# A fifth pair of high and low weight tiles, and a smaller scratch for GpSimd's DMA descriptors

## The chip, the cores and the metric

The kernel runs on one core of one Trainium2 chip. The metric is the time of one execution in microseconds (us) on the device. A core has five engines, each with an instruction stream of its own that it works through in the order written: TensorE (PE in the profile, with PEld for its loads of stationary weights), VectorE (DVE), ScalarE (ACT), GpSimd (POOL) and SyncE (SP), which here only issues DMAs. Engines wait for each other through semaphores. Matmul results go to PSUM; weights and activations lie in SBUF, on chip.

## The reference

Two layers of a decoder trunk on 256 tokens of width 1024, all in float32. Each layer normalizes x, projects it, runs four causal token mixers side by side (stick-breaking attention, RWKV-7, block attention with rotary embedding, HGRN2), gates their projected outputs and adds an output projection, then a SwiGLU feed-forward part:

```python
for layer in range(DEPTH):
    h = rms_norm(x, norm1_g[layer])
    y_sb, y_rwkv, y_moba, y_hgrn = four_mixers(h @ w_in[layer])   # each (256, 256)
    merged = None
    for n, y_n in enumerate((y_sb, y_rwkv, y_moba, y_hgrn)):
        gate = jax.nn.sigmoid(cols(GATE_OFF + n * D_MODEL, D_MODEL))
        term = gate * (y_n @ w_branch[layer, n])
        merged = term if merged is None else merged + term
    x = x + merged @ w_out[layer]
    h2 = rms_norm(x, norm2_g[layer])
    x = x + (jax.nn.silu(h2 @ w_ffn_gate[layer]) * (h2 @ w_ffn_up[layer])) @ w_ffn_down[layer]
return rms_norm(x, final_g)
```

The RWKV-7 recurrence is computed in two chunks of 128 steps per head. Each chunk needs the inverse of a unit triangular 128x128 matrix; the kernel builds it up from blocks of 16.

## The kernel before, in words

**Weights.** Every weight matrix is read once, in tiles of 128x1024 (512 KB). SyncE issues a load into one of four `raw` tiles (L133). A matmul on full float32 is replaced by three on a shorter format: ScalarE rounds the tile to a high part `hi` (L128), VectorE subtracts to get the low part `lo` (L129), and TensorE adds hi·h_hi, hi·h_lo and lo·h_hi (`mm3`, recorded under L80). One pair of hi and lo tiles therefore stands between the two splitting engines and TensorE; the pool has `spl` such pairs, four before. A pair is free again when TensorE's last matmul with that weight tile is done. Some weights are split ahead of their stage into tiles of other pools (`prefetch`, names c and y).

**Stages.** A layer runs through `phase` (projections, mixers, gates and branch projections), `merge` (the output projection) and `ffn`. In `phase` the work comes as units (projections, gate and branch tiles, which keep TensorE busy) and streams (the mixers, whose short steps alternate between engines). `drive` interleaves them by a running estimate of TensorE's time; that estimate counts matmuls alone and does not read the pools' sizes. The order on each engine is then settled when the program is built: the framework places instructions engine by engine as buffers and inputs become available in its own plan, so the number of buffers can change the order on ScalarE, VectorE and SyncE. Once built, the order is fixed.

**PSUM.** Projections and gates accumulate into `pa`, of which there are three. Each is released by the engine that reads it last: for HGRN2's last projection (`use_n`) ScalarE copies one half (L810), takes the sigmoid of the other (L811), and VectorE multiplies (L812), which frees the buffer. A gate's `pa` is freed by ScalarE's sigmoid (L1011); a branch's `pa` by VectorE's multiplication with the gate (L1029, L1031).

**The inverse.** VectorE fills the triangular matrices LB by predicated copies (L542). GpSimd sends each chunk to DRAM (L548, tensor `flat`), ScalarE's queue fetches the diagonal blocks of 16 back with one matrix to a partition (L564), VectorE inverts them in three levels of multiplications and sums (L591, L594, tile `yb`), GpSimd sends the result to DRAM (L599, `tri`) and ScalarE's queue fetches it back (L602). L602 waits, in ScalarE's stream, for the landing of `tri`. GpSimd issues six DMAs in the whole program, four to `flat` and two to `tri`. For GpSimd's DMAs the descriptors are written by software into a scratch at the bottom of SBUF; its size per partition is an argument of the program's constructor and is 16384 bytes where none is given.

Of the kernel before, what the change touches and what calls it, by code (L numbers as in the profile page):

```python
# [39 lines left out]
SWAP = [*range(8, 16), *range(8), *range(16, 32)]  # L40
P_MU, P_W0, P_A0, P_KK, P_KA, P_RK, P_V0, P_LB, NPAR = 0, 8, 10, 12, 14, 16, 18, 20, 24

NB = dict(raw=4, spl=4, h4=2, p=11, y=8, c1=8, xy=4, b1=5, c2=4, b2=2, h1=4, h2=3, gt=4, pa=3, p1=2, p2=2, p3=1)


@with_exitstack
def trunk(ctx, tc, x, w_t, w_n, w_br, w_out, w_gu, w_dn, par, lora, rows, gains, consts, masks, out):
# [9 lines left out]
    def sb(tag, width, dt=F32):  # L57
        return mx.tile([128, width], dt, name=tag, tag=tag, bufs=NB[tag])

    def ps(tag):  # L60
        return psum.tile([128, 512], F32, name=tag, tag=tag, bufs=NB[tag])

# [68 lines left out]
    def load_raw(src):  # L131
        raw = sb("raw", 1024)
        nc.sync.dma_start(raw, src)  # L133
        return raw
# [3 lines left out]
    def weight(key):  # L138
        name, idx = key[0], key[1:]
        raw = early.pop(key, None)  # L140
        if raw is None:
            raw = load_raw(WSRC[name][idx])
        w = (mx.tile([128, 1024], F32R, name="hi", tag="hi", bufs=NB["spl"]),
             mx.tile([128, 1024], F32R, name="lo", tag="lo", bufs=NB["spl"]))
        if guard and guard[2]:
# [860 lines left out]
    def gate_unit(h, l, n, f, gt):  # L1006
        gt[n, f] = []

        def use(t, p):
            g = sb("gt", 512)  # L1010
            nc.scalar.activation(g, p, AF.Sigmoid)  # L1011
            gt[n, f].append(g)
        return proj_N(h, [("n", l, 2 + 2 * n + f, c) for c in range(4)], use)

    def branch_unit(l, n, f, cnt, yT, gt, mg, mT):
        i = cnt[f]
        cnt[f] += 1
        w = weight(("br", l, n, f))
        y = yT[n][0]
        gs = gt.pop((n, f))  # L1020
        for t in range(2):
            p = ps("pa")
            for hp in range(2):
                mm3(p, (y[0][:, hp, t * 128:(t + 1) * 128], y[1][:, hp, t * 128:(t + 1) * 128]),
                    cut(w, slice(hp * 512, (hp + 1) * 512)), hp == 0, hp == 1)
            g = gs[t]
            if i == 0:
                mg[f, t] = sb("p", 512)
                nc.vector.tensor_tensor(mg[f, t], g, p, op=OP.mult)  # L1029
            else:  # L1030
                nc.vector.tensor_tensor(g, g, p, op=OP.mult)  # L1031
                e = nc.vector if i == 3 else nc.gpsimd
                e.tensor_tensor(mg[f, t], mg[f, t], g, op=OP.add)  # L1033
            if t == 0 and f == 1 and i == 3:
                assert cnt[0] == 4
                yield from flip_unit(0, mg, mT)
            yield
# [13 lines left out]
    def phase(hr, g, l, ws):  # L1051
# [4 lines left out]
        def add(gen, ready=yes):  # L1056
            units.append((ready, gen))
# [39 lines left out]
        for n in (0, 2, 3, 1):  # L1097
            for f in range(2):
                add(lambda n=n, f=f: gate_unit(h, l, n, f, gt), lambda: len(gt) < NB["gt"] // 2)
                add(lambda n=n, f=f: branch_unit(l, n, f, cnt, yT, gt, mg, mT),  # L1100
# [195 lines left out]
```

## Time and profile before

| | |
|---|---|
| three runs | 924.91, 926.62, 926.95 us; median 926.62 |
| profiled execution | 924.23 us, of which 922.4 us from the first to the last instruction |
| TensorE busy | 905.6 us (98%), 5902 matmuls |
| VectorE busy | 650.8 us (71%) |
| ScalarE busy | 475.4 us (52%) |
| GpSimd busy | 88.2 us (10%) |
| DMA | 158.11 MB, mean 171 GB/s; mean granted TensorE clock 0.998 |

In the rows of a timeline the columns are: start in us from the span's start, length in us, engine and line, operation, tiles (written <- read), shape, and the number of merged instructions; in brackets the idle time of the engine before it and what ended that. An engine name with q is its sequencer, which issues a DMA and leaves the engine idle. A matmul's row says which tile is moving and which is stationary: `pa<-hi,h` moves a hi tile through stationary h. Matmuls overlap and their ends are modelled, so the distance of starts is the better measure there. In a table of waits the columns are who waited for whom, the sum in us, how often, and the longest.

### The profile page before, as it was taken

To read this page: it belongs to the slowest core of one execution; us is meant where nothing else is said; L and a number is where in the kernel's file an instruction comes from. 1 tells how busy PE (TensorE), PEld (TensorE's weight loads), DVE (VectorE), ACT (ScalarE), POOL (GpSimd) and SP (SyncE) were. 2 spreads that over 40 slices of the span, in tenths; PEclk is the share of its full clock that TensorE was granted. 3 is DMA by queue.
4 is the path that set the end of the run, shared out by engine and by line. 5 is a ranking of instruction groups with operands and counts; after the bars stand their busy time and mean duration, and the time that the engine had idled before them with its cause. 6 is when DMAs were issued, how large, how long until landed. Compare 5 with 4: busy or idle time off the path is not lost.

```text
span 922.4 us, 15005 instructions
## 1 busy us (share of the span) xinstructions
PE 905.6 (98%) x5902; PEld 758.9 (82%) x5902; DVE 650.8 (71%) x957; ACT 475.4 (52%) x726; POOL 88.2 (10%) x100
## 2 busy tenths in 40 slices
PE   8999999999999999999999999999999999999996
PEld 5999777778788888888889987777788888888885
DVE  6667877887766666668567778768778566666665
ACT  6564385345635445556355646644455445545453
POOL 3012100323000000000000211033130000000000
PEclk9999999999999999999999999999999999999999
DMA  8644453435754565567434544533377356556551
GB/s 311 221 149 152 121 174 126 135 131 184 257 199 140 181 198 189 183 208 268 141 116 160 163 138 152 174 104 117 116 218 256 106 188 207 191 182 192 183 183 46
DMA packets 48536, 158.11 MB, mean 171 GB/s; under 512 B 9393, under 2 KB 9777, under 8 KB 48466
## 3 DMA queue, kind: packets, MB, share of 16 engines
q1 hardware_dynamic: 43632, 155.19, 51.6%
q10 hardware_dynamic: 4450, 0.79, 0.5%
q0 software_dynamic: 384, 1.18, 0.4%
q8 instruction: 46, 0.75, 0.3%
q14 instruction: 24, 0.20, 0.1%
HBM read 154.91 MB, written 2.23 MB: 170 GB/s over the span
## 4 chain that ended last, share of the span: by engine, by line
PE 84%; DVE 9%; issue 2%; ACT 2%; DMA 1%; POOL 1%; ACTq 0%; POOLq 0%; DVEq 0%
PE pa L80 58%; PE p L80 23%; DVE lo L129 2%; PE pa L89 1%; PE p L89 1%; DVE b L542 1%; ACT hi L128 1%; DMA flat<-b 1%; DVE b L867 1%; DVE b L965 1%; DMA raw<-in_w_out_dram 1%; PE pa L196 0%; DVE xy L591 0%; DVE c L981 0%; DVE c L980 0%
## 5 line engine op out<-in xcount | busy, mean ns | idle before, releaser
L129 DVE TENSOR_TENSOR lo<-raw,hi 128x1024 fp32r<-128x1024 f32 x268 | 330.9, 1240 | 154.5 <-ACT hi L128 150.9
L128 ACT CAST hi<-raw 128x1024 fp32r<-128x1024 f32 x268 | 279.3, 1049 | 234.3 <-PE pa L80 109.3
L80 PE MATMUL pa<-h,hi 128*128 128x256 f32 (+1 forms) x1280 | 278.0, 339 | 0.0
L80 PEld LDWEIGHTS pa<-h,hi 128*128 128x128 f32 x1280 | 216.1, 190 | 24.5 <-issue 2.0
L80 PE MATMUL pa<-hi,h 128*128 128x512 f32 x576 | 193.2, 400 | 3.1 <-DVE p L812 3.1
L80 PE MATMUL pa<-h,lo 128*128 128x256 f32 x960 | 180.1, 283 | 0.0
L80 PEld LDWEIGHTS pa<-h,lo 128*128 128x128 f32 x960 | 148.8, 191 | 6.9 <-issue 0.7
L80 PEld LDWEIGHTS pa<-hi,h 128*128 128x128 f32 x576 | 108.2, 188 | 29.6 <-DVE p L812 4.0
L80 PE MATMUL p<-hi,c 128*128 128x512 f32 (+1 forms) x352 | 113.5, 394 | 0.0
L80 PE MATMUL pa<-lo,h 128*128 128x512 f32 x288 | 112.9, 392 | 0.0
L80 PEld LDWEIGHTS p<-hi,c 128*128 128x128 f32 x352 | 66.1, 189 | 15.1 <-DVE c L129 0.6
L80 PE MATMUL p<-lo,c 128*128 128x512 f32 (+1 forms) x176 | 69.3, 394 | 0.0
L80 PEld LDWEIGHTS pa<-lo,h 128*128 128x128 f32 x288 | 54.2, 188 | 9.6
L263 POOL TENSOR_TENSOR rs<-rs,half 128x1 f32<-128x1 f32 x10 | 5.9, 594 | 471.4 <-DVE rs L262 471.4
L80 PE MATMUL pa<-hi,y 128*128 128x512 f32 x128 | 44.0, 399 | 0.1
L80 PE MATMUL p<-hi,b 128*128 128x512 f32 x128 | 41.6, 396 | 0.3 <-DVE b L129 0.2
L80 PEld LDWEIGHTS p<-lo,c 128*128 128x128 f32 x176 | 33.2, 189 | 6.7
L1033 POOL TENSOR_TENSOR p<-p,gt 128x512 f32<-128x512 f32 x16 | 30.9, 1950 | 39.4 <-DVE gt L1031 31.9
L340 DVE TENSOR_TENSOR gt<-gt,pa 128x256 f32<-128x256 f32 x80 | 33.1, 413 | 0.0
L128 ACT CAST c<-xy 128x512 fp32r<-128x512 f32 x20 | 12.4, 620 | 39.7 <-DVE xy L1136 39.7
L80 PEld LDWEIGHTS pa<-hi,y 128*128 128x128 f32 x128 | 24.0, 188 | 6.7 <-issue 0.7
L339 ACT COPY gt<-pa 128x256 f32<-128x256 f32 x80 | 29.1, 364 | 0.0
(278 smaller groups left out, 941.6 us busy)
## 6 DMA issues: line engine op xcount, KB each, us to landing
raw<-in_w_gu_dram SPq DMA_DIRECT2D x88, 512.0 KB, 3.9
raw<-in_w_n_dram SPq DMA_DIRECT2D x80, 512.0 KB, 3.6
raw<-in_w_dn_dram SPq DMA_DIRECT2D x44, 512.0 KB, 3.5
raw<-in_w_t_dram SPq DMA_DIRECT2D x40, 512.0 KB, 3.5
raw<-in_w_br_dram SPq DMA_DIRECT2D x16, 512.0 KB, 3.7
raw<-in_w_out_dram SPq DMA_DIRECT2D x16, 512.0 KB, 4.3
b<-in_gains_dram SPq DMA_DIRECT2D x4, 512.0 KB, 5.5
flat<-b POOLq DMA_DIRECT2D x4, 256.0 KB, 3.3
```

The source lines that it names most:

```text
L80: nc.tensor.matmul(o, l, r, start=start, stop=stop)
L89: nc.tensor.transpose(o, i, ident)
L128: a = nc.scalar.copy(dst[0], src)
L129: return a, (eng or nc.vector).tensor_tensor(dst[1], src, dst[0], op=OP.subtract)
L263: nc.gpsimd.tensor_tensor(dst, dst, half[:, :dst.shape[-1]], op=OP.pow)
L339: nc.scalar.copy(dst, p[:, 256:512])
L340: nc.vector.tensor_tensor(dst, dst, p[:, 0:256], op=OP.add)
L542: nc.vector.copy_predicated(dst[:, u::2], over(armask, 2), g2d(p[u], 2))
L867: nc.vector.tensor_tensor(qv, qv, t4[s, :, :, 0:1].to_broadcast([64, 2, 2 * nb, hb]), op=OP.mult)
L965: nc.vector.tensor_tensor_scan(kb, kb, reset[t][:, ::-1], 1.0, op0=OP.mult, op1=OP.add)
L1033: e.tensor_tensor(mg[f, t], mg[f, t], g, op=OP.add)
```

## The change

Two arguments change. The pool of hi and lo tiles gets five pairs for four, which takes another 8192 bytes of each SBUF partition (two tiles of 1024 values of 4 bytes). The scratch for GpSimd's descriptors goes from 16384 to 8192 bytes of each partition. No instruction is added or removed; the `raw` pool keeps its four tiles.

```diff
-NB = dict(raw=4, spl=4, h4=2, p=11, y=8, c1=8, xy=4, b1=5, c2=4, b2=2, h1=4, h2=3, gt=4, pa=3, p1=2, p2=2, p3=1)
+NB = dict(raw=4, spl=5, h4=2, p=11, y=8, c1=8, xy=4, b1=5, c2=4, b2=2, h1=4, h2=3, gt=4, pa=3, p1=2, p2=2, p3=1)
...
-    nc = _bacc.Bacc("TRN2", target_bir_lowering=False, num_devices=1)
+    nc = _bacc.Bacc("TRN2", target_bir_lowering=False, num_devices=1, dynamic_dma_scratch_size=8192)
```

The order on TensorE and GpSimd stays the same, instruction by instruction. On ScalarE, VectorE and SyncE it moves. From the first layer's start on, one more weight tile stands split ahead of TensorE at the same place. Three places matter below; each occurs in both layers alike.

On ScalarE, at the end of the inverse in the first layer (L602 fetches the inverse back from `tri`; L810 and L811 read HGRN2's last projection from `pa`, once for each half of the tokens):

```order
 L128 CAST y<-p_780 128x512
 L128 CAST hi<-raw 128x1024 x3
+L602 DMA h_1372<-tri 128x8x16
 L810 COPY p<-pa 128x256
 L811 ACTIVATE p<-pa 128x256
-L602 DMA h_1372<-tri 128x8x16
 L810 COPY p<-pa 128x256
 L811 ACTIVATE p<-pa 128x256
```

The fetch of `tri` moved ahead of the first pair L810, L811; before, it stood between the two pairs.

On VectorE, the last part of the same inverse (its products and sums are L591 and L594; the last L594 of the piece completes `yb`), before:

```order
L594 TENSOR_REDUCE yb<-xy 64x4x4 x2
L129 TENSOR_TENSOR lo<-raw,hi 128x1024
L591 TENSOR_TENSOR xy<-yb,h_1120 64x512
L542 COPY_PREDICATED b_1178<-mk,p_1179 128x2x256
L542 COPY_PREDICATED b_1178<-mk,p_1180 128x2x256
L594 TENSOR_REDUCE h_1250<-xy 64x64
L591 TENSOR_TENSOR xy<-h_1250,yb 64x512
L129 TENSOR_TENSOR lo<-raw,hi 128x1024
L594 TENSOR_REDUCE yb<-xy 64x8x8
L129 TENSOR_TENSOR lo<-raw,hi 128x1024
L812 TENSOR_TENSOR p<-p,pa 128x256
```

and after:

```order
L591 TENSOR_TENSOR xy<-yb,h_1120 64x512
L983 TENSOR_TENSOR c_1155<-c_1155,p 128x512
L594 TENSOR_REDUCE h_1250<-xy 64x64
L129 TENSOR_TENSOR lo<-raw,hi 128x1024
L591 TENSOR_TENSOR xy<-h_1250,yb 64x512
L542 COPY_PREDICATED b_1178<-mk,p_1179 128x2x256
L542 COPY_PREDICATED b_1178<-mk,p_1180 128x2x256
L594 TENSOR_REDUCE yb<-xy 64x8x8
L129 TENSOR_TENSOR lo<-raw,hi 128x1024 x3
L812 TENSOR_TENSOR p<-p,pa 128x256
```

Before, three of these subtractions to lo stand ahead of the last L594 (one more of them above the rows shown, between two steps of the inverse); now one does, and two have moved behind it. The total up to L812 is the same four.

On ScalarE, near the end of the first layer's gates and branches (L1011 is the sigmoid of a gate, which frees a `pa`; y is a weight split ahead):

```order
 L128 CAST c_2582<-raw 128x512
-L128 CAST hi<-raw 128x1024 x2
-L1011 ACTIVATE gt<-pa 128x512 x2
-L128 CAST hi<-raw 128x1024 x4
+L128 CAST hi<-raw 128x1024 x3
+L1011 ACTIVATE gt<-pa 128x512 x2
+L128 CAST hi<-raw 128x1024 x3
 L128 CAST y<-raw 128x512 x2
```

A third weight tile is rounded ahead of the two sigmoids.

## The prediction

> **What bounds the kernel now.** I read the page's busy times first, then TensorE's waits, then the stages around the longest of them.
>
> ```profile
> span 922.4 us, 15005 instructions
> PE 905.6 (98%) x5902; PEld 758.9 (82%) x5902; DVE 650.8 (71%) x957; ACT 475.4 (52%) x726; POOL 88.2 (10%) x100
> ...
> PE pa L80 <- DVE p L812: 3.1, 2, 1.6
> PE p L80 <- DVE c L868: 0.9, 1, 0.9
> ...
> PE pa L80 <- DVE lo L129: 0.4, 1, 0.4
> PE p L80 <- DVE b L129: 0.2, 1, 0.2
> ```
>
> TensorE is busy for 905.6 of 922.4 us, so the matmul stream sets the time, and only 16.8 us are idle. The stages, by windows (columns: window, length, busy time and number of instructions of PE, PEld, DVE, ACT, POOL, then clock, DMA share and GB/s), show where:
>
> ```profile
> 0.00:17.00 17.00, 13.99 (x59) 8.34 (x60) 10.11 (x18) 9.87 (x20) 7.27 (x17) 1.00 0.88 315
> 94.00:110.00 16.00, 14.63 (x79) 11.01 (x75) 15.96 (x29) 4.41 (x6) 2.73 (x3) 1.00 0.34 105
> 300.00:440.00 140.00, 140.00 (x730) 119.42 (x730) 94.53 (x118) 74.01 (x108) 0.00 (x0) 1.00 0.62 202
> 547.00:562.00 15.00, 13.44 (x66) 10.12 (x65) 14.97 (x27) 3.83 (x5) 2.95 (x4) 1.00 0.31 95
> 914.00:922.40 8.40, 0.88 (x8) 0.68 (x6) 3.26 (x8) 2.35 (x7) 0.55 (x1) 0.83 0.34 126
> ```
>
> The head loses 3.0 us and the tail 7.5; no weight tile of the hi and lo pool decides either (the head splits into other tiles, the tail is the last normalization). The feed-forward stage loses nothing: 140.00 of 140.00. What is left for this change lies almost wholly in two stages, one in each layer, in which VectorE is full (15.96 of 16, 14.97 of 15) and TensorE waits for L812. A late lo tile of this pool costs 0.4 us, once. So the fifth pair has little to win as a buffer; what it does to the order on the engines decides.
>
> **The change part by part.** *The smaller scratch.* GpSimd's issues and their queue:
>
> ```profile
> q0 software_dynamic: 384, 1.18, 0.4%
> ...
> 83.02 0.97 POOL L548 DMA_DIRECT2D flat<-b  x1 [2.33 <-DVE b L542]
> 86.49 0.76 POOL L548 DMA_DIRECT2D flat<-b  x1 [2.50 <-DVE b L542]
> flat<-b POOLq DMA_DIRECT2D x4, 256.0 KB, 3.3
> ```
>
> The second `flat` is issued 3.5 us after the first, which lands in about 3.3. Even if the first had to have left the scratch, it nearly has. I take nothing; the upper bound is the third rival.
>
> *The end of the inverse, layer 0.* These rows of the timeline hold the chain:
>
> ```profile
> 94.45 1.21 DVE L129 TENSOR_TENSOR lo<-raw,hi 128x1024 fp32r<-128x1024 f32 x1
> 101.87 1.20 DVE L129 TENSOR_TENSOR lo<-raw,hi 128x1024 fp32r<-128x1024 f32 x1
> 103.00 1.03 DVE L591 TENSOR_TENSOR xy<-yb,h 64x512 f32<-64x512 f32 x1
> 106.88 1.21 DVE L129 TENSOR_TENSOR lo<-raw,hi 128x1024 fp32r<-128x1024 f32 x1
> 108.01 0.67 DVE L594 TENSOR_REDUCE yb<-xy 64x64 f32<-64x512 f32 x1
> 109.74 0.40 DVE L812 TENSOR_TENSOR p<-p,pa 128x256 f32<-128x256 f32 x1
> 110.20 0.50 PE L80 MATMUL pa<-hi,h 128*128 128x512 f32 x1 [1.57 <-DVE p L812]
> ...
> 105.07 0.37 ACT L810 COPY p<-pa 128x256 f32<-128x256 f32 x1 [0.30 <-PE pa L80]
> 105.34 0.39 ACT L811 ACTIVATE p<-pa 128x256 f32<-128x256 f32 x1
> 112.79 0.41 ACTq L602 DMA_DIRECT2D h<-tri  x1
> 113.25 0.37 ACT L810 COPY p<-pa 128x256 f32<-128x256 f32 x1 [7.52 <-DMA tri<-yb]
> 113.52 0.39 ACT L811 ACTIVATE p<-pa 128x256 f32<-128x256 f32 x1
> 113.94 0.42 DVE L812 TENSOR_TENSOR p<-p,pa 128x256 f32<-128x256 f32 x1 [2.21 <-ACT p L811]
> ```
>
> Today the first pair L810, L811 ends at 105.73, long before L812 gets its turn on VectorE at 109.74; TensorE goes on 0.46 us after L812's start. The second pair stands behind L602, which holds ScalarE's stream until `tri` has landed, 112.79; nobody on TensorE misses it. With the new order the first pair stands behind L602 too, and behind it L812, and behind that TensorE.
>
> VectorE has no idle time in this stretch, and two of the three lo rows move behind the last L594. A lo row occupies 1.13 us, from its start to the next one's (101.87 to 103.00, 106.88 to 108.01). So `yb` ends 2.26 us sooner: 108.68 - 2.26 = 106.4. From the end of `yb` to L602 it took 112.79 - 108.68 = 4.1 us (GpSimd's issue, landing of `tri`), so L602 issues at 110.5. L810 follows 0.46 later and L811 0.27 after that, ending at 111.64; L812 starts 0.03 later (113.91 to 113.94), at 111.67. The two lo rows behind `yb` are over by then: with the one that already stood there they are three, 3.4 us, to 109.8. TensorE goes on at 111.67 + 0.46 = 112.1 and not at 110.20: **+1.9 us**. Bounds: if `tri` landed 0.8 us faster (the difference to layer 1, below), +1.1; if VectorE gained nothing before `yb`, +1.9 + 2.26 = +4.2.
>
> *The same, layer 1.*
>
> ```profile
> 559.55 0.67 DVE L594 TENSOR_REDUCE yb<-xy 64x64 f32<-64x512 f32 x1
> 563.52 0.38 ACTq L602 DMA_DIRECT2D h<-tri  x1
> 563.94 0.38 ACT L810 COPY p<-pa 128x256 f32<-128x256 f32 x1 [6.66 <-DMA tri<-yb]
> 561.74 0.50 PE L80 MATMUL pa<-hi,h 128*128 128x512 f32 x1 [1.56 <-DVE p L812]
> ```
>
> Here `yb` ends at 560.22 and L602 comes 3.3 us later. Moved by 2.26: 557.96, L602 at 561.26, L810 at 561.68, L811 to 562.34, L812 at 562.37, TensorE at 562.8 for 561.74: **+1.1 us**. Bounds: +0.3 with 0.8 us taken off as above, +1.9 with the slower landing of layer 0.
>
> *The two sigmoids behind a third rounding.*
>
> ```profile
> 231.12 1.05 ACT L128 CAST hi<-raw 128x1024 fp32r<-128x1024 f32 x1 [2.43 <-DMA raw<-in_w_n_dram]
> 233.82 1.05 ACT L128 CAST hi<-raw 128x1024 fp32r<-128x1024 f32 x1 [1.65 <-DMA raw<-in_w_n_dram]
> 234.78 1.07 ACT L1011 ACTIVATE gt<-pa 128x512 f32<-128x512 f32 x2
> 236.62 1.05 ACT L128 CAST hi<-raw 128x1024 fp32r<-128x1024 f32 x1 [0.77 <-DMA raw<-in_w_n_dram]
> 235.28 0.64 PE L80 MATMUL pa<-hi,y 128*128 128x512 f32 x2
> ```
>
> ScalarE waits here for loads into `raw`, which still has four tiles. The branch matmuls that start at 235.5 (the second of the merged row at 235.28) take the `pa` that the first sigmoid frees at about 235.3, with 0.2 us to spare. If the third rounding kept its time, 236.62, the sigmoids would slip by 236.62 + 0.95 - 234.78 = 2.8 us (0.95 is the distance of a rounding to what follows it, 233.82 to 234.78), and TensorE would stand still for 2.6. But the loads come sooner as well: a `raw` tile is free when its split is done, and on VectorE the splits ahead of these now pass one lo row (1.13 us) and a split of half a tile (half as many elements, an estimated 0.6), 1.7 us. Then the sigmoids slip by 1.1 and TensorE waits 0.9. Bounds: 0, if the load comes sooner by the whole 2.8, and 2.6. I take the middle between 0 and the worked 0.9, **+0.5 us** a layer and +1.0 for both, because a load that also waited for SyncE's earlier ones gains less or more than the split did.
>
> *What the fifth pair saves.* The one wait for lo, 0.4 us at 120.66, and the 0.2 us for L129 at the start of `merge`: **-0.6 us**. The bound below is 0. Upwards, weight loads on TensorE also wait in places that matmuls cover:
>
> ```profile
> PEld p L80 <- ACT hi L128: 2.1, 6, 0.4
> PEld pa L80 <- DVE lo L129: 1.5, 3, 0.8
> ```
>
> If all of that were won, -3.6 us. I stay at -0.6, since the same waits on PE's own rows sum to no more.
>
> Here a rule speaks against my reading. The Trainium skill, "Perfetto Trace Analysis", section "Optimization Strategy", says that the same gap repeating on the engine that should be full can mean too little SBUF for the next tile, so more buffers. By it the sum would be -0.6 alone, or down to -3.6. The trace shows no such repeating gap for this pool: one wait of 0.4 us in 922.
>
> The sum: 1.9 + 1.1 + 1.0 - 0.6 = **+3.4 us**. Against the profiled execution, 924.23 us (1.8 us around the span), that is 927.6. The median of the three runs lies 2.4 us above the profiled one, so I forecast 926.62 + 3.4 = **930.0 us**.
>
> **The rivals.** *Faster: L602 no longer holds anything.* If `tri` landed before L810 could start anyway, at 105.07, L812 would run as soon as the sigmoid is done, both waits of 1.56 us would vanish, and with the 0.6 saved the time would be 926.62 - 3.1 - 0.6 = 922.9. For that `yb` would have to end by about 101; the two lo rows give 2.26 us of the 7.7 needed. It also needs L812 ahead of the lo rows, and it stands behind three. The milder form, in which the inverse's end costs its low bounds, the sigmoids nothing, and the waits of weight loads all turn into gain (1.1 + 0.3 - 3.6), comes out at 924.4. Together 12%.
>
> *No difference.* All terms at their low ends: 1.1 + 0.3 + 0 - 0.6 = +0.8, 927.4. For it: L602's time hangs on two DMA landings, which differ by 0.8 us between the layers. Against: it needs every term to fall on the same side. 22%.
>
> *Much slower: the scratch.* If GpSimd had to wait for room in the smaller scratch, each second `flat` would be late by up to a landing, 3.3 us a layer; ScalarE's L564 waits for it with all roundings behind, and it would be on top of the +3.4: 926.62 + 3.4 + 6.6 = 936.6. It decides from the point at which one `flat` does not fit beside the last. The Trainium skill, "DMA: Bandwidth & Descriptors", section "Terms", gives a descriptor as 16 bytes in rings in SBUF; by that 8192 bytes hold 512 of them, and the 128 x 4 rows of a `flat`, spread over 16 engines, are an estimated 32 for each. By that nothing waits; no run shown has a smaller scratch. With it I count the sigmoids' upper bound (2.6 a layer: 926.62 + 1.9 + 1.1 + 5.2 - 0.6 = 934.2). Together 9%.
>
> That the change does nothing is ruled out for the order, which is settled when the program is built.
>
> **How the numbers follow.** The forecast, slower by 1.9 to 5.5 us, has 57%, the larger loss 9%, no difference 22%, faster 12%. 0.2% (1.9 us) is about what a measurement of this kernel can tell from no change. So faster 0.12, same 0.22, slower 0.66. The likeliest case's own range is 928.3 to 932.5. For 8 in 10 I add the lower half: down to 925.5, which takes in no difference and a slight gain, up to 933.0.
>
> **What would show it.** In the changed profile L602 should stand before both L810s, at about 110.5, with the wait for `tri` of some 5 us ending at the first L810; TensorE's wait for L812 should be about 3.5 us in layer 0 and 2.6 in layer 1, for 1.57 and 1.56. The end of `yb` should be near 106.4. A wait on PE for L1011 of about half a microsecond should be new near 237 and 692. The feed-forward windows should be unchanged at full TensorE. I am wrong if the waits for L812 do not grow, if `yb` ends no sooner (then the loss is larger), or if GpSimd's second `flat` comes later than 3.5 us after the first.

## The result, and the profile after

The changed kernel takes 936.7 us (median of four runs, 935.67 to 938.6) against 926.79 us for the kernel before (924.91 to 927.78). The ratio is 1.0113, with a 95% interval of 1.0096 to 1.0130. I had said 930.0 us, 925.5 to 933.0. The sign was right. The size was not, and neither was the cause.

First, how much of the difference between the two profiled executions (936.01 and 924.23 us, 11.8 us apart) belongs to the change. These rows of TensorE's timeline are the start of its steady work, in the kernel before:

```profile
12.75 1.22 PE L80 MATMUL pa<-y,h 128*128 128x512 f32 x4
```

in the changed kernel:

```profile
15.49 1.24 PE L80 MATMUL pa<-y,h 128*128 128x512 f32 x4
```

and in a run with the order of the kernel before and only the scratch halved (the first experiment below):

```profile
15.49 1.23 PE L80 MATMUL pa<-y,h 128*128 128x512 f32 x4
```

The head of the program takes 2.7 us more in some profiled executions than in others, whatever the kernel: it is short in the kernel before and in the run with L606 back, long in the changed kernel and in the run with the scratch alone. In the long ones TensorE's matmuls go at half pace for longer; the eight of L89 ahead of these rows take 1.04 us in the kernel before (from 7.23) and 1.91 in the changed one (from 9.53). (The trace's record of the granted clock begins at 4.79 us before and at 12.57 after; ahead of it the views read 1.00.) I therefore count from this row to the end of the span: 922.4 - 12.75 = 909.7 us before and 934.2 - 15.49 = 918.7 after. **The change costs 9.0 us there**, close to the 9.9 between the medians.

The page's busy times and TensorE's waits of the changed kernel:

```profile
span 934.2 us, 14965 instructions
PE 912.4 (98%) x5902; PEld 762.2 (82%) x5902; DVE 653.4 (70%) x957; ACT 475.3 (51%) x726; POOL 87.1 (9%) x100
...
PE pa L80 <- ACT gt L1011: 5.5, 2, 2.8
PE pa L80 <- DVE p L812: 3.1, 2, 1.6
...
PE p L80 <- DVE c L868: 0.9, 1, 0.9
...
PE pa L80 <- DVE gt L1031: 0.3, 1, 0.3
```

The waits for L812, on which most of my sum rested, are what they were: 3.1 us in all. New is a wait of 2.8 us for L1011, a gate's sigmoid on ScalarE, once in each layer. TensorE is also busy for 6.8 us more with the same 5902 matmuls. Of these, 3.2 lie in the head (13.81 us busy up to 15.49, against 10.62 up to 12.75 before); the rest says that some matmuls of the steady work ran slower as well. (The instructions that the page counts are 40 fewer than before; those are semaphore waits.)

The chain that leads to the new wait, in layer 0, from the timelines of SyncE, VectorE, ScalarE and TensorE:

```profile
110.25 2.60 SPq L133 DMA_DIRECT2D raw<-in_w_n_dram  x3
...
108.39 0.69 DVE L594 TENSOR_REDUCE yb<-xy 64x64 f32<-64x512 f32 x1
108.98 3.51 DVE L129 TENSOR_TENSOR lo<-raw,hi 128x1024 fp32r<-128x1024 f32 x3
112.55 0.42 DVE L812 TENSOR_TENSOR p<-p,pa 128x256 f32<-128x256 f32 x1
112.89 0.75 DVE L929 TENSOR_TENSOR c<-p,cn 128x256 f32<-128x256 f32 x2
118.41 0.69 DVE L606 TENSOR_TENSOR xy<-h,mk 128x512 f32<-128x512 f32 x1 [4.77 <-DMA h<-tri]
119.02 0.68 DVE L990 TENSOR_REDUCE mxs<-c 128x4 f32<-128x512 f32 x1
119.62 0.41 DVE L812 TENSOR_TENSOR p<-p,pa 128x256 f32<-128x256 f32 x1
119.95 0.16 DVE L991 TENSOR_SCALAR mxs<-mxs 128x4 f32<-128x4 f32 x1
...
111.37 0.45 ACTq L602 DMA_DIRECT2D h<-tri  x1
111.86 0.37 ACT L810 COPY p<-pa 128x256 f32<-128x256 f32 x1 [4.30 <-DMA tri<-yb]
...
120.19 1.28 ACT L994 ACT_TABLE_LOAD   x1 [6.18 <-DVE mxs L991]
...
123.04 2.93 ACT L128 CAST hi<-raw 128x1024 fp32r<-128x1024 f32 x3
125.98 1.28 ACT L1011 ACT_TABLE_LOAD   x1
127.28 1.09 ACT L1011 ACTIVATE gt<-pa 128x512 f32<-128x512 f32 x2
...
113.03 0.50 PE L80 MATMUL pa<-hi,h 128*128 128x512 f32 x1 [1.61 <-DVE p L812]
...
127.93 0.50 PE L80 MATMUL pa<-hi,y 128*128 128x512 f32 x1 [2.78 <-ACT gt L1011]
...
129.24 0.63 PE L80 MATMUL pa<-lo,y 128*128 128x512 f32 x1
129.66 0.63 PE L80 MATMUL pa<-hi,y 128*128 128x512 f32 x1
130.09 0.63 PE L80 MATMUL pa<-hi,h 128*128 128x512 f32 x1
```

Read it so. Three subtractions to lo stand back to back at 108.98, so three raw tiles come free in a row, and SyncE issues three loads of 512 KB from 110.25 to 112.85. In the midst of them, at 111.37, L602 fetches the inverse's blocks into `h`. VectorE then meets **L606**, the first reader of `h`, and stands still for 4.77 us. Behind L606 stand L990 and L991, the maximum of the block attention's softmax, which have nothing to do with the inverse. ScalarE waits 6.18 us for that maximum, then does its exponentials (L994), three roundings, a table load and the sigmoids of L1011. These free the `pa` for which TensorE has been waiting since 125.15. In layer 1 it is the same: L606 starts at 573.59 after 4.50 us of idle time, and TensorE waits 2.77 us to 583.11.

The fetch itself became slow. Its time from issue to landing (min, median, max), before, where the trace has the landing of layer 1 alone:

```profile
DMA to landing us min/median/max: 3.2/3.2/3.2
```

and after, of both layers:

```profile
DMA to landing us min/median/max: 6.7/6.9/7.0
```

The last three of TensorE's rows above show the slow matmuls: they start 0.42 and 0.43 us apart, where such matmuls start 0.23 apart elsewhere in the stage. The windows of the changed kernel around the stall (columns as in the prediction) give a clock to it:

```profile
124.90:128.00 3.10, 0.32 (x4) 0.08 (x2) 2.98 (x4) 3.07 (x5) 0.00 (x0) 1.00 0.59 168
128.00:132.40 4.40, 4.40 (x12) 3.23 (x12) 3.41 (x4) 2.83 (x4) 0.00 (x0) 0.61 0.78 281
132.40:140.00 7.60, 7.60 (x43) 5.98 (x43) 3.60 (x6) 4.77 (x11) 0.00 (x0) 1.00 0.50 153
```

After the stall the granted clock is 0.61 in the mean over 4.4 us, with TensorE busy throughout, and 1.00 behind that.

### The profile page after: what moved, and what is told of

It reads as the page before. It is cut to its first block, busy times and chain, and to the rows that moved or that the text cites. A ratio compares the mean times of both kernels' runs of the same rounds, so it can differ in the third digit from the quotient of the medians.

```text
span 934.2 us, 14965 instructions
## 1 busy us (share of the span) xinstructions
PE 912.4 (98%) x5902; PEld 762.2 (82%) x5902; DVE 653.4 (70%) x957; ACT 475.3 (51%) x726; POOL 87.1 (9%) x100
## 4 chain that ended last, share of the span: by engine, by line
PE 79%; DVE 9%; DMA 4%; issue 3%; ACT 3%; POOL 1%; SPq 0%; ACTq 0%; POOLq 0%; DVEq 0%
PE pa L80 55%; PE p L80 22%; DVE lo L129 2%; ACT hi L128 1%; PE pa L89 1%; DMA raw<-in_w_gu_dram 1%; PE p L89 1%; DMA h<-tri 1%; DMA xr<-in_x_dram 1%; DMA lora<-in_lora_dram 1%; DMA flat<-b 1%; DVE b L867 1%; DVE b L965 1%; DVE b L542 0%; DVE xy L591 0%
## 5 line engine op out<-in xcount | busy, mean ns | idle before, releaser
L1033 POOL TENSOR_TENSOR p<-p,gt 128x512 f32<-128x512 f32 x16 | 27.9, 1756 | 43.7 <-DVE gt L1031 36.1
```

## The experiments

The theory after this reading, T in the expectations: the loss comes from the *order on VectorE*, L606 with its late fetch ahead of L990, L991 and the second L812. Rival R1 is the halved scratch, rival R2 the step of my forecast (L602 ahead of both L810). The edits that move an instruction use `issue_after(x)`, which makes what stands in its block follow x on x's engine and changes nothing else; `mark` only holds recorded instructions. Ratios are to the kernel before, run beside each.

**The scratch alone.**

```diff
-    nc = _bacc.Bacc("TRN2", target_bir_lowering=False, num_devices=1)
+    nc = _bacc.Bacc("TRN2", target_bir_lowering=False, num_devices=1, dynamic_dma_scratch_size=8192)
```

> Four pairs as before, and only the descriptor scratch halved; every engine's order is that of before. Theory T (the loss comes from the order on VectorE: L606, which waits for the fetch of the inverse's blocks, now stands ahead of L990, L991 and the second L812): no difference, 926 to 928 us, the fetch into h lands in about 3.2 us as before. Rival R1 (the halved scratch slows GpSimd's DMAs or the start of the program): 930 to 937 us, with the landing of tri or of h slower than before's 3.8 and 3.2 us, or a longer head.

Measured: 926.73 us, ratio 1.0000 (0.9988 to 1.0013). The fetch into `h` lands in 2.3 us. Two of R1's signs are there, a long head and a `tri` that lands in 3.8 and 4.6 us, but R1 put the time at 930 to 937 us. The scratch costs nothing that the time shows: R1 falls.

**L606 back behind the softmax's maximum.** `mark[0]` is L991, `mark[3]` the second L812.

```diff
-            nc.vector.tensor_tensor(y.rearrange("p a (k t) -> p a k t", k=8),
...
+            with tc.issue_after(mark[0]), tc.issue_after(mark[3]):
+                nc.vector.tensor_tensor(y.rearrange("p a (k t) -> p a k t", k=8),
```

> The changed kernel with L606 held behind L991 and the second L812 on VectorE, as it stood before; the other four engines keep the changed kernel's order, L602 ahead of both L810 included. T: PE's wait for the gates of L1011 (2.8 us twice) and the slow matmuls behind it go, about 4.5 us a layer: 927 to 929 us. R1 (scratch) and rival R2 (L602 ahead of both L810 and L811 on ScalarE, the step of the forecast): 934 to 937 us, as the changed kernel.

Measured: 927.41 us, ratio 1.0001 (0.9984 to 1.0019). The whole loss is gone, with five pairs, the small scratch and ScalarE's new order all still there. Its VectorE:

```profile
110.71 0.69 DVE L990 TENSOR_REDUCE mxs<-c 128x4 f32<-128x512 f32 x1
111.44 0.17 DVE L991 TENSOR_SCALAR mxs<-mxs 128x4 f32<-128x4 f32 x1
...
114.50 0.69 DVE L607 TENSOR_TENSOR xy<-h,mk 128x512 f32<-128x512 f32 x1 [2.57 <-DMA h<-tri]
```

(The added line makes L606 into L607.) The fetch is as slow as in the changed kernel, 6.1 and 7.4 us, and VectorE still waits for it. But the maximum is now ahead of the wait, and TensorE waits for nothing from 112 to 135 us. No wait for L1011 is left.

**L602 back between the two pairs on ScalarE.** `mark[4]` is the first L811.

```diff
-        nc.scalar.dma_start(cb, bass.AP(tensor=tri.tensor, offset=tri.offset, ap=[[16, 128], [2048, 8], [1, 16]]))
+        with tc.issue_after(mark[4]): nc.scalar.dma_start(cb, bass.AP(tensor=tri.tensor, offset=tri.offset, ap=[[16, 128], [2048, 8], [1, 16]]))
```

> The changed kernel with only L602 moved back between the two pairs of L810 and L811 on ScalarE, as before; on VectorE the first L606 still stands ahead of L991 and the second L812. T: the wait for h stays ahead of the softmax, 934 to 938 us. R2: back to 926 to 930 us.

Measured: 936.53 us, ratio 1.0092 (1.0063 to 1.0121). Undoing the move on which my forecast was built leaves the loss in place: the interval overlaps that of the changed kernel. Counted from the start of the steady work, this profiled execution takes 917.0 us, 1.7 of the 9.0 less; the stalls are 1.82 and 2.45 us for 2.78 and 2.77. Two rows show why the loss stays, VectorE's and TensorE's:

```profile
114.35 0.69 DVE L606 TENSOR_TENSOR xy<-h,mk 128x512 f32<-128x512 f32 x1 [3.51 <-DMA h<-tri]
...
122.96 0.50 PE L80 MATMUL pa<-hi,y 128*128 128x512 f32 x1 [1.82 <-ACT gt L1011]
```

In this program L606 stands between L990 and L991, and that is enough. R2 falls as the cause of more than these 1.7 us.

**L602 late.** The same edit with the second L811. L602 then comes behind the exponentials and L606 behind L997.

> The changed kernel with L602 held behind the second L811; the program then also puts L602 behind the exponentials of L994, and L606 behind L997 on VectorE. T: no wait for h stands ahead of the softmax, and L810 to L812 no longer wait for tri, so that PE's 1.6 us at L812 shrink too: 923 to 927 us, unless the inverse, some 8 us later, becomes what PE waits for at L631 (then 928 to 934 us). R1: 934 to 937 us.

Measured: 925.84 us, ratio 0.9993 (0.9974 to 1.0012). The loss is gone again, by another way of getting L606 out of the path; the later inverse costs nothing. But the two waits at L812, which I had expected to shrink, are still 1.6 us each, though L811 ends at 108.53 here and waits for no DMA. What holds L812 back is the three subtractions to lo that stand ahead of it, in this kernel as in the changed one.

**L606 between L991 and the second L812.** This asks which of the two late instructions matters; `mark[0]` is L991, and the edit is shown against the run with L606 back.

```diff
-            with tc.issue_after(mark[0]), tc.issue_after(mark[3]):
+            with tc.issue_after(mark[0]):
```

> The changed kernel with L606 behind L991 but still ahead of the second L812 on VectorE. If the loss runs over the softmax (L991, then L994, then L1011): 926 to 929 us. If it runs over the second L812, which frees the tile of pa: 934 to 937 us, with TensorE waiting for L812 a third and a fourth time.

Measured: 927.73 us, ratio 1.0005 (0.9991 to 1.0019). The loss runs over the maximum and the exponentials to L1011, not over the second L812.

**The loads held back until the fetch has landed.** This leaves every engine's order as in the changed kernel, L606 ahead of L991 included, but for one small copy added on SyncE, and takes away the loads beside the fetch.

```diff
-        nc.scalar.dma_start(cb, bass.AP(tensor=tri.tensor, offset=tri.offset, ap=[[16, 128], [2048, 8], [1, 16]]))
+        nc.scalar.dma_start(cb, bass.AP(tensor=tri.tensor, offset=tri.offset, ap=[[16, 128], [2048, 8], [1, 16]])); wt[:] = nc.sync.dma_start(dram.tile([1, 16], F32, name="seen"), cb[0:1, 0, :]).ins, 3
...
-        nc.sync.dma_start(raw, src)
+        with ExitStack() as es: wt[1] > 0 and es.enter_context(tc.issue_after(wt[0])); wt[1] -= 1; nc.sync.dma_start(raw, src)
```

> The changed kernel with the next three loads of raw held on SP until the fetch into h has landed (a copy of 64 bytes out of h, issued on SP ahead of them, waits for it); every other engine's order is the changed kernel's, L606 ahead of L991 included. If the loads beside it make the fetch slow: it lands in 2 to 4 us as in the kernel before, not in 6.7 to 7.3; L606 starts 3 to 4 us sooner, and the wait at L1011 and the slow matmuls go: 926 to 930 us, unless the held loads make TensorE wait for lo. If the fetch is slow by itself (its 64-byte pieces, the halved scratch): 6.5 to 7.5 us again and 935 to 938 us.

Measured: 927.57 us, ratio 0.9994 (0.9979 to 1.0008). SyncE, VectorE and the landing of the fetch:

```profile
113.49 0.31 SPq L602 DMA_DIRECT2D seen<-h  x1
113.91 3.96 SPq L133 DMA_DIRECT2D raw<-in_w_n_dram  x4
...
113.50 0.73 DVE L606 TENSOR_TENSOR xy<-h,mk 128x512 f32<-128x512 f32 x1
114.16 0.67 DVE L990 TENSOR_REDUCE mxs<-c 128x4 f32<-128x512 f32 x1
...
DMA to landing us min/median/max: 2.2/2.2/2.2
```

L606 waits for nothing. So the loss needs both: the reader of the fetch ahead of the softmax, *and* the fetch among the loads. Either one taken away brings the time back.

**The stall filled with work.** Are the slow matmuls a consequence of TensorE standing idle? The four transposes ahead of the stall are done six times over into the same tile (`n` is 6 for the first softmax of each layer and 1 elsewhere; the estimate that `drive` goes by is corrected, so that the interleaving stays).

```diff
-            for a in range(4):
+            for a in [*range(4)] * n:
                 tr(p[:, a * 128:(a + 1) * 128], att[:, a, b * 128:(b + 1) * 128])
```

> The changed kernel with the four transposes of L89 for the first softmax done six times over into the same tile, 20 more of about 0.11 us each: they fill most of the 2.8 us in which TensorE waits for L1011 and change nothing else in any engine's order. If the slow matmuls behind the stall come from TensorE standing idle: no 0.43 us steps behind it, PEclk 1.0 there, 1.4 to 1.8 us saved a layer, 933 to 934 us. If they come from the loads or from chance: the steps stay and the time is 936 to 938 us.

Measured: 934.87 us, ratio 1.0086 (1.0068 to 1.0103). The window that had the clock of 0.61 above:

```profile
124.20:128.00 3.80, 3.20 (x27) 2.87 (x26) 3.67 (x4) 3.77 (x6) 0.00 (x0) 1.00 0.57 202
128.00:132.40 4.40, 4.40 (x29) 3.10 (x28) 3.05 (x4) 2.48 (x4) 0.00 (x0) 1.00 0.86 277
```

29 matmuls start in it in place of 12, at full clock, and the loads beside them are no fewer. From the end of the stall to the next group of small matmuls (`p<-c,p`) it takes 130.39 - 127.42 = 2.97 us, against 132.47 - 127.93 = 4.54 in the changed kernel; in layer 1 2.97 against 4.29. The halved clock costs 1.6 and 1.3 us. Beside its own runs of the kernel before the loss falls from 9.9 to 7.6 us between the medians, so 2.3 of these 2.9 come back, less than I had expected; the intervals of the two ratios overlap, and it is the profile that shows the effect. In layer 1 the profile names a reason for the rest: the fetch took 8.0 us this time (6.5 in the other layer; 6.7 to 7.0 in the changed kernel), and what followed it was later.

**L812 ahead of the lo parts, with five pairs.** The experiments point at L812's 3.1 us, which both kernels lose. Here the lo parts of the next three weights follow the first L812, L602 follows the second L811 and L606 follows L997.

```diff
-            nc.vector.tensor_tensor(gs[:, t], gs[:, t], p[:, 256:512], op=OP.mult)
+            e = nc.vector.tensor_tensor(gs[:, t], gs[:, t], p[:, 256:512], op=OP.mult); guard[:] = [e.ins, e.ins, 3 - t] if t == 0 else guard
...
```

> The changed kernel with the order around L812 mended: the next low parts of L129 behind the first L812, L602 behind the second L811, L606 behind L997. T: TensorE's 1.6 us at L812 go in both layers, beside the 2.8 us at L1011 and the slow matmuls: 922.5 to 925 us, and the fetch into h lands faster than 6.7 us since the raw loads start later. If the low parts now come too late: new waits of PE for lo of 1 us and more, 925 to 929 us.

Measured: 927.5 us, ratio 1.0001 (0.9991 to 1.0012). **The same with four pairs and the full scratch:**

> The kernel before, with four pairs and the full scratch, and the same three edits of the order as the run with L812 first. If the fifth pair is worth what the forecast gave it (0.6 us) or nothing: 922.5 to 926 us, within 1 us of its five-pair twin. If the fifth pair is what lets the order be mended: 926 us and more, with waits for lo.

Measured: 924.52 us, ratio 0.9981 (0.9970 to 0.9992). Both expectations are missed: the five pairs gain nothing, and the twins are 3.0 us apart. TensorE's waits with five pairs:

```profile
PE pa L80 <- ACT gt L1011: 1.4, 2, 1.2
PE pa L80 <- DVE gt L1031: 1.2, 2, 0.7
...
PE pa L80 <- DVE lo L129: 0.8, 2, 0.4
```

and with four:

```profile
PE pa L80 <- DVE lo L129: 2.1, 2, 1.2
```

The wait for L812 is gone in both. With four pairs 2.1 us of waits for lo take its place; with five, 3.4 us for L1011, L1031 and lo. The wait for L1011 is again one of ScalarE's order: with five pairs four roundings stand between the exponentials and L1011, three of which wait for a load or for lo themselves, and L1011's table load starts 7.8 us after the last exponential has ended; with four pairs three stand there and it is 5.5 us. The waits explain 1.3 of the 3.0 us between the medians. I leave the rest open.

**Four pairs with L812 first, and the freed 8 KB as two more raw tiles.** Against the kernel before, beside the edits of the order:

```diff
-NB = dict(raw=4, spl=4, h4=2, p=11, y=8, c1=8, xy=4, b1=5, c2=4, b2=2, h1=4, h2=3, gt=4, pa=3, p1=2, p2=2, p3=1)
+NB = dict(raw=6, spl=4, h4=2, p=11, y=8, c1=8, xy=4, b1=5, c2=4, b2=2, h1=4, h2=3, gt=4, pa=3, p1=2, p2=2, p3=1)
...
-    nc = _bacc.Bacc("TRN2", target_bir_lowering=False, num_devices=1)
+    nc = _bacc.Bacc("TRN2", target_bir_lowering=False, num_devices=1, dynamic_dma_scratch_size=8192)
```

> The run with four pairs and L812 first, and the 8 KB a partition that the halved scratch frees spent on two more raw tiles (six) in place of the fifth pair. If the freed space is worth something as raw tiles: the waits of ScalarE's roundings for raw (1.6 and 0.7 us near 118 and 120 us) go, 922 to 924 us. If TensorE doesn't wait for these: 924 to 925.5 us, as with four raw tiles; if the earlier loads run beside the fetch and slow it: 926 us and more, with L607 late.

Measured: 924.81 us, ratio 0.9972 (0.9959 to 0.9986). Its interval overlaps that of the run with four raw tiles, so the raw tiles are not shown to bring anything. Both versions with four pairs and L812 first are faster than the kernel before, by 0.2 to 0.3%, and than the changed kernel, by 1.3%. From the start of the steady work to the end their profiled executions take 907.2 and 907.9 us, against 909.7 in the kernel before and 909.8 with five pairs and L812 first.

## Why the prediction was wrong

**The inverse's end, +1.9 and +1.1 us: wrong, about 0 and 0.** The part on VectorE was right: `yb` ends at 108.39 + 0.69 = 109.08, or 106.3 with the 2.7 us of the head taken off, for 106.4 predicted; and L602 does stand ahead of both L810, with 4.30 us of idle time there. The term then took the time from the end of `yb` to L602 from the kernel before, 4.1 us. It was 2.3: `tri` landed in 2.0 us in both layers and not in 3.0 to 3.8. A load had started ahead of `tri` before (108.11, `tri` at 108.98) and now starts behind it (110.25, `tri` at 109.38); in every run without a load that close ahead of it, it lands in 2.0 us, in the two with one (the kernel before and the scratch alone) in 3.0 to 4.6. So the second operand of the first L812 was there at 112.52, within 0.03 us of its turn on VectorE behind the three lo parts (112.49), and TensorE's wait stayed at 1.61. My lower bound, 0.8 us off the landing, was too narrow.

**The omitted step decides: L606.** I followed L602 on ScalarE to who stands behind the *issuing* instruction, L810 to L812, and never to who stands behind the *reader* of what it fetches. The rows of VectorE's order that I showed end at L812; L606 stands three instructions further down, ahead of L990 and L991, where it had stood behind them. That was to be seen before any run. What could only be bounded was how long it would wait. The fetch took 3.2 us in the kernel before, and at that L606 would have started near 114.6 and L991 near 116, some 4 us sooner than they did. That is more than the stall of 2.78, so I take it that there would have been none at L1011. The run with the loads held comes close to that case, with a fetch of 2.2 us: 927.57 us. Measured: 2.78 + 2.77 us of stall, and 1.6 + 1.3 us of slow matmuls behind it, together 8.4 of the 9.0 us.

**The sigmoids behind a third rounding, +0.5 us each: too high.** TensorE has no wait at the sigmoids behind the third rounding (241.52 and 699.79): my lower bound, 0, is what came. The new wait of 0.3 us at L1031 in layer 1 ends at 688.37, 11 us ahead of them, and is another one. The mechanism came up where I had not looked: in the run with L812 first and five pairs.

**The fifth pair's own gain, -0.6 us: the waits go, a gain is not shown.** The waits for lo of 0.4 us and for b of 0.2 us are gone in the changed kernel. With L606 back behind the maximum the five pairs measure 1.0001 against the kernel before (0.9984 to 1.0019, some 1.7 us either way), and 0.6 us of waits for L1031 stand in their place.

**The rivals.** The scratch, priced at 936.6, came nearest to the measured number and is ruled out as its cause by the first experiment; that its second `flat` comes 3.48 us after the first (85.79 to 89.27) said so already. "No difference" would have been the right forecast if the order had kept L606 where it was. The feed-forward stage was unchanged, as expected: 140.00 of 140.00 us from 300 to 440. The two statements of the likeliest range differ by a slip: 928.3 to 932.5 is slower by 1.7 to 5.9 us, not by 1.9 to 5.5; nothing hangs on it.

## What to carry to other kernels

When a change reorders engines, follow each moved DMA to the instruction that *reads* what it brings, and ask what stands behind that reader on its engine. A buffer count is also a schedule: one more buffer lets several loads start together, and a small latency-bound transfer that now falls among them can take twice as long. Price a stall of TensorE at its length and, where it leaves TensorE less than half busy in a window of 3.4 us, at up to 1.7 us more for the halved clock behind it; the next section works this out.

## What the runs showed of the hardware that I had not expected

**A short stall halves the clock for one window of 3.41 us.** Between the head and the tail, TensorE's granted clock fell five times in the twelve traces of this document. Each time the trace's record of the clock has 0.50 for 3.41 us and 1.00 on both sides; the means of 0.61 above are mixtures of the two. The stretches at full clock between two changes are whole multiples of 3.41 us (in the changed kernel 34, 132 and 101 of them). So the clock is set for windows of one fixed length, and their borders stay where they are whenever a stall comes. What decides is how busy TensorE was in the window before. The changed kernel, the window with most of the stall of 2.78 us and the next one:

```profile
125.21:128.62 3.41, 0.69 (x3) 0.60 (x4) 3.26 (x4) 3.38 (x5) 0.00 (x0) 1.00 0.60 173
128.62:132.03 3.41, 3.41 (x10) 2.63 (x9) 2.45 (x3) 2.21 (x3) 0.00 (x0) 0.50 0.72 278
```

the same around the stall of 1.82 us in the run with L602 back, which lies in one window as a whole:

```profile
120.90:124.31 3.41, 1.59 (x9) 1.14 (x7) 2.83 (x3) 3.38 (x6) 0.00 (x0) 1.00 0.59 191
124.31:127.72 3.41, 3.41 (x12) 2.27 (x12) 2.96 (x3) 1.52 (x3) 0.00 (x0) 0.50 0.92 330
```

and around the stall of 1.81 us in layer 1 of the run with the loads held (562.98 to 564.80), which a border cuts at 563.15:

```profile
563.15:566.56 3.41, 1.76 (x8) 1.47 (x9) 3.35 (x7) 2.14 (x5) 0.74 (x1) 1.00 0.19 19
566.56:569.97 3.41, 3.41 (x17) 2.83 (x16) 3.41 (x6) 2.72 (x8) 2.08 (x2) 1.00 0.86 303
```

The five windows ahead of a drop had TensorE busy for 0.69, 1.09, 1.08, 1.59 and 1.44 us of 3.41, with stalls of 2.78, 2.77, 2.45, 1.82 and 1.97 us; no window with 1.76 us or more was followed by one. The limit lies between 47% and 52% of the window. The run with the stall filled agrees: its emptiest window has 1.8 us, and its clock stays at 1.00. At half clock 3.41 us cost at most 1.7, which fits the 1.6 and 1.3 measured. The Trainium skill, "TensorE: Matmul & The Clock Gate", section "Why this matters for your kernels", asks for no idle gaps above some 3 us between bursts of matmuls. By that none of these stalls would have cost more than its length; here 1.82 us was enough, and the measurement decides. The same page of the Trainium skill, section "What's actually happening", tells of a free-running window over which activity is judged; the traces agree, and show that such a window need not be idle from end to end.

**A small fetch among large loads takes two to three times as long.** The 64 KB of `h` in pieces of 64 bytes landed in 2.2 us with no load beside it, in 2.3 to 3.2 us with one (the kernel before, the scratch alone, L812 first with five pairs), in 4.0 to 4.2 us in the runs with L602 late and with four pairs and L812 first, and in 5.9 to 8.0 us where L602 fell among three loads of 512 KB issued 1.1 us apart (the changed kernel and the runs with L606 back, L606 between, L602 back and the stall filled). The Trainium skill, "DMA: Bandwidth & Descriptors", section "Queues, rings and completion order", says that each DMA engine takes turns between the queues it has work for, a whole packet at a time. That agrees with the direction; no run here shows the turns themselves.
